# A streaming-encoder block: the residual placed in the output first, the last step added onto it by accumulating transfers

## The chip, the cores and the metric

The kernel runs on one core of one Trainium2 chip. The metric is the device time of one execution in microseconds. Times of the profile are those of one profiled execution, counted from the start of its span.

The engines are named as in the profile: PE multiplies matrices (PEld loads its weights), DVE is the vector engine, ACT the scalar engine, POOL is GpSimd, and SP mostly starts transfers. SPq, ACTq and POOLq are the DMA queues of the engines that issue the transfers.

## The reference, cut to what matters

```python
for l in range(DEPTH):                                   # one layer
    h = rmsnorm(x, norm_mix_pre[l])
    proj = h @ w_in[l]                                   # pool branch, GLU pair, two gates
    branch_a, branch_b = pool_mixer(...), conformer_conv(...)
    merged = sigmoid(g_a) * branch_a + sigmoid(g_b) * branch_b
    x = x + rmsnorm(merged @ w_o[l], norm_mix_post[l])   # x1 below
    h = rmsnorm(x, norm_mlp_pre[l])
    f = square(relu(h @ w_up[l])) @ w_down[l]
    x = x + rmsnorm(f, norm_mlp_post[l])                 # the output
# rmsnorm(y, g) = y * rsqrt(mean(y*y) + 1e-6) * g
```

The input has 2048 tokens of 1024 channels in float32; the MLP is 4096 wide. The value of `x` after the first half of the layer is called x1. The output is x1 plus the normalised MLP result, times a gain per channel.

The kernel doesn't normalise x1 ahead of `w_up`. Since relu and square pass a positive factor of a token through as its square, it multiplies unnormalised x1 and puts the token's factor into the last normalisation instead. That last normalisation then needs, per token, a function of the mean square of x1: the code calls it the floor (the "MLP scale"), which stands in for the 1e-6.

## The kernel before, in words

**Tiling.** A tile is 128 x 1024 float32 (512 KB). Tokens are split into two blocks of 1024 (`b`), each block into two halves of 512 (`t`), each half into four groups of 128 tokens (`g`). Up to the MLP, data lie with channels on the partitions. The last product, `down`, has tokens on the partitions: its results are 128 tokens by 512 channels (`m` is the half of the channels, `h` the pair of groups; one accumulator tile holds two groups of 128 tokens side by side for one `m`).

**Products.** Every large product is computed as seven products of halves instead of eight (index `i` from 1 to 7; some need sums of weight tiles and of token tiles, some don't), and every operand is split into a rounded high part (`wh`, a cast on ACT) and a low part (`wl`, a subtraction on DVE), with three matmuls each. In `down` the 4096 inputs are taken in four slabs; slab 3 is the last (`LAST`). A job of `down` is one index `i` for one block `b`: 24 matmuls for each of the two `h`.

**Stages.** Input projections and convolution for block 0, then 1; merge and `w_o`; `up` for block 0 and, after `w_o` of block 1, `up` for block 1; then `down`, slab 0 to slab 3. In the profile `down` runs from about 1541 us to the end, and its last slab from about 2000 us.

**What sets the order.** The Python program is run once and gives each engine its own list of instructions; waits on semaphores tie the lists together. Work beside the matmuls is written as generators in lanes: `Lane(rate, ...)` takes `rate` steps of its generators at each call of `bg()`, which comes once for each `h` of a job; `yield n` in a generator waits `n` steps. `with tc.high_priority(...)` puts instructions ahead in the engine's list.

**The parts the change touches.**

- `mlp_scale` (line 1312) and `scales` (1578): while `up` of block 1 runs, x1 is read back with channels on the partitions (`fo<-x1d`), squared on ACT (line 579), added on DVE, and summed over the channels by matmuls against a column of 1/1024 (`rb<-inv_d,fo`, line 458). The result is the floor of each group of tokens.
- `last_weights` (line 1559): also beside `up` of block 1, the weights of the last slab are read, the sums for i = 5, 6, 3, 7 are formed and stored (`wsum`), and the low part of every weight tile is computed and stored (`lows`). In the last slab `part` (line 1634) loads the tile, casts its high part, and loads its low part (`wl<-lows`).
- `turned` (line 1771): beside slabs 0 to 2, x1 is read (two loads per piece, `tr<-x1d`), transposed by DVE in squares of 32 x 32 (line 1785), and written with tokens as rows to an internal buffer (four stores per piece, `x1t<-tr`). All six go through POOL's queue. There are 16 pieces.
- `Finish`: one per (block, half). When an accumulator is ready, ACT sums its squares (line 1812), and DVE multiplies it by the gain (`big<-big,ws`). When all four are ready, a chain of small DVE operations (`root`, `root_dve`) gives the factor per token; for each group of 128 tokens the row tile of x1 is fetched (`big<-x1t`), and DVE computes y times factor plus x1 in two halves (line 1832), and the row tile is stored (`put`, line 1839: POOL's queue for block 0, SP's for block 1). The last `Finish` does the same in `at_end` as its matmuls end, with stores of 256 KB on SP's queue (line 1888).

The program is built with `dynamic_dma_scratch_size=1024` (line 2046), the space it sets aside for the descriptors of transfers that POOL issues. Both versions have this line.

Of the kernel before, what the change touches and what calls it, by code (L numbers as in the profile page):

```python
# [67 lines left out]
def block_kernel(  # L68
# [124 lines left out]
    fd, x1t = {}, {(b, t): dram("x1t", (T, D)) for b in range(NB) for t in (0, 1)}  # L193
# [958 lines left out]
    floor = {}  # L1152
# [158 lines left out]

    def mlp_scale(b, buf):

        st = None
        for t in (0, 1):
            sq = Squares(buf)
            for c in range(0, CPS, 2):
                x = [mk(*buf) for _ in (0, 1)]
                for i in (0, 1):
                    load(x[i], x1d[b, c + i, t])  # L1320
                yield 1
                sq.add(x[0])
                sq.add(x[1])
            yield 1
            ss = sq.total()
            yield 2
            if st is None:
                st = root_psum()
            root_acc(st, ss, inv_d, t * G)
        yield 1  # L1330
        m = small("sa", 2 * G)
        nc.vector.tensor_scalar(
            m, st[:, : 2 * G], EPS, SQ * EPS**0.5, op0=ALU.add, op1=ALU.mult
        )
        e = p_const.tile([P, 2 * G], F32, tag=f"e{b}", name=f"e{b}")
        mul(e, m, m)
        for t in (0, 1):
            floor[b, t] = e[:, t * G : (t + 1) * G]
        yield
# [230 lines left out]
    def last_weights():  # L1570
# [11 lines left out]
        keys = [(o, i) for o in (0, 1) for i in DOWN]  # L1582
        for (o, i), got in ahead_by_one(keys, fetch_one):
# [15 lines left out]
            hi, lo = split(t, *TR)  # L1599
            yield 1  # L1600
            lows[i, o] = dram("lows")
            load(lows[i, o], f32(lo))

    def scales():
        for b in range(NB):
            yield from mlp_scale(b, (p_fo, "fo"))


    def weights_down(s):
# [27 lines left out]
        def part(i, o):  # L1637
            with tc.high_priority(offset=AHEAD):
                if s < LAST:
                    return split_w(source(i, o))  # L1640
                if (i, o) in wsum:
                    t = mk(p_wr, "wr")
                    load(t, wsum[i, o])
                else:
                    t = source(i, o)
                hi, lo = mk(p_wh, "wh", F32R), mk(p_wl, "wl", F32R)
                nc.scalar.copy(hi, t)
                load(f32(lo), lows[i, o])
                return hi, lo
# [120 lines left out]

    def turned():
        for b in range(NB):
            for t in (0, 1):
                to = x1t[b, t].rearrange("(n tb i) (q k j) -> n q i tb k j", n=2, i=32, q=4, j=32)
                for c in (0, 2):
                    for n in (0, 1):
# [7 lines left out]
                        yield 4  # L1784
# [9 lines left out]
                        yield  # L1794

# [3 lines left out]
    class Finish:  # L1799
# [16 lines left out]
        def gain(self, m, h):  # L1816
# [3 lines left out]
            row = gains[0][:, m * T : (m + 1) * T].unsqueeze(1).to_broadcast([P, 2, T])  # L1820
            mul(two(y), two(y), row)

        def root(self, lo, hi):
            ss = small("st", hi - lo)
            add(ss, self.ss[:, lo:hi], self.ss[:, G + lo : G + hi])
            return root_dve(ss, floor[self.b, self.t][:, lo:hi], 1.0 / D)

        def cell(self, g, r, y):
            x = self.x[g]
            for m in (0, 1):  # L1830
                s = slice(m * T, (m + 1) * T)
                nc.vector.scalar_tensor_tensor(x[:, s], y[m], r, x[:, s], op0=ALU.mult, op1=ALU.add)

        def parts(self, g):
            s = slice(g % 2 * T, (g % 2 + 1) * T)
            return [self.ready[m, g // 2][:, s] for m in (0, 1)]

        def put(self, g):
            (nc.gpsimd if self.b == 0 else nc.sync).dma_start(
                out[self.b, self.t, g], self.x[g]  # L1840
            )

        def steps(self, lag):
# [5 lines left out]
            for g in range(3):  # L1849
                self.fetch(g)  # L1850
# [3 lines left out]
            for g in range(G):  # L1854
                if g + 3 < G:
                    self.fetch(g + 3)
                self.cell(g, r[:, g : g + 1], self.parts(g))
                self.put(g)
                yield

        def last_steps(self):
            for n, k in enumerate(((1, 0), (1, 1))):
# [4 lines left out]
                self.fetch(2 * n)  # L1867
                yield
                self.fetch(2 * n + 1)
                yield  # L1870

        def at_end(self, h, c, ps):
            y = tr()
            halves = [slice(i * T, (i + 1) * T) for i in (0, 1)]

            def arrive(gg):
                s = halves[gg]
                mark(add(c[:, s], c[:, s], ps[gg]))
                self.squares(0, h, c[:, s], gg)
                mul(y[:, s], c[:, s], gains[0][:, :T])  # L1880

            def leave(g, r):
                to = out[self.b, self.t, g]
                part = [y[:, halves[g % 2]], self.ready[1, h][:, halves[g % 2]]]
                x = self.x[g]
                for m, s in list(enumerate(halves))[::-1]:
                    nc.vector.scalar_tensor_tensor(x[:, s], part[m], r, x[:, s], op0=ALU.mult, op1=ALU.add)
                    load(to[:, s], x[:, s])
# [63 lines left out]
    for n, (s, i, b) in enumerate(jobs):  # L1952
# [17 lines left out]
        if n == 1:  # L1970
            lanes.append(Lane(2, turned()))
# [82 lines left out]
```

## Time and profile before

| what | value |
|---|---|
| median of 3 runs | 2153.35 us (2151.98 to 2154.61) |
| profiled execution | 2155.38 us, of it span 2153.6 us and 1.8 us around it |
| mean granted clock of PE | 0.996 |
| PE busy | 2130.3 us, 99% of the span |
| DVE busy | 1717.0 us, 80% |
| ACT busy | 1024.5 us, 48% |
| POOL busy | 74.8 us, 3% |
| PE's last matmul ends | 2141.0 us |
| DVE's last operation ends | 2150.2 us |

An engine is busy while it runs an instruction of its own; issuing a transfer counts as busy for POOL but not for SP. A row of a timeline gives the start, the length, the engine, the line of the kernel, the operation, what it writes and reads, the count, and in brackets the idle time ahead of it with what ended it. A row of DMA issues gives the queue, the count, the size of each transfer and the median time from its issue to its landing.

### The profile page before, as it was taken

What the parts mean: (1) busy time and instruction counts of PE and PEld (TensorE: products, weight loads), DVE (VectorE), ACT (ScalarE), POOL (GpSimd) and SP (SyncE); (2) the same over time, 40 slices, a digit from 0 to 9 for tenths busy, and PEclk for the clock granted to TensorE, in tenths of its full rate; (3) what the DMA queues carried; (4) which work ended last, traced back from release to release, by engine and by line L of the source; (5) the groups of instructions that cost most, each with busy time, mean ns of one, the idle gap of its engine ahead of it and who ended that gap; (6) DMA issues with size and microseconds to landing.
All of it is one profiled execution on the core that took longest, in us unless ns stands there. A gap on an engine that the chain in (4) does not pass through costs nothing.

```text
span 2153.6 us, 24989 instructions
## 1 busy us (share of the span) xinstructions
PE 2130.3 (99%) x9424; PEld 1758.8 (82%) x9424; DVE 1717.0 (80%) x1669; ACT 1024.5 (48%) x1109; POOL 74.8 (3%) x131
## 2 busy tenths in 40 slices
PE   9999999999999999999999999999999999999997
PEld 8788888888888888888888888888888888888886
DVE  8999788999779999998768766876745667688558
ACT  6444453334534755446645676665544322223343
POOL 0000000000000000000000000000011111100000
PEclk9999999999999999999999999999999999999999
DMA  4789999688897787335596787995977657564568
GB/s 178 262 309 329 342 356 317 223 292 290 307 345 282 248 305 292 149 118 223 200 382 211 248 293 268 338 334 192 366 264 264 246 197 253 180 221 164 198 228 338
DMA packets 164617, 568.04 MB, mean 264 GB/s; under 512 B 19984, under 2 KB 24208, under 8 KB 164496
## 3 DMA queue, kind: packets, MB, share of 16 engines
q1 hardware_dynamic: 142736, 490.93, 63.4%
q10 hardware_dynamic: 12672, 46.14, 5.5%
q0 software_dynamic: 9088, 29.37, 3.9%
q8 instruction: 74, 1.21, 0.2%
q14 instruction: 47, 0.39, 0.1%
HBM read 370.71 MB, written 195.65 MB: 263 GB/s over the span
## 4 chain that ended last, share of the span: by engine, by line
PE 85%; DVE 8%; DMA 3%; issue 2%; ACT 1%; SPq 0%; DVEq 0%; ACTq 0%
PE up L252 28%; PE down L1708 26%; PE wo L252 7%; PE glu L252 4%; PE B L252 4%; PE gb L252 4%; PE A L252 4%; PE ga L252 3%; DVE y L910 3%; PE pool L252 3%; PE rb L1708 1%; DVE tr L120 1%; DVE wl L123 1%; DMA kept<-ws 1%; PE rb L458 1%
## 5 line engine op out<-in xcount | busy, mean ns | idle before, releaser
L252 PE MATMUL up<-big,wh 128*128 128x512 f32 x1792 | 481.0, 390 | 1.4 <-DVE big L123 0.8
L252 PEld LDWEIGHTS up<-big,wh 128*128 128x128 f32 x1792 | 335.7, 188 | 72.5 <-DVE big L123 1.1
L209 ACT CAST wh<-wr 128x1024 fp32r<-128x1024 f32 x167 | 175.6, 1052 | 305.8 <-PE up L252 70.0
L910 DVE SCALAR_TENSOR_TENSOR y<-v,cst,y 128x1024 f32<-128x1024 f32 x240 | 307.1, 1280 | 2.4
L1708 PE MATMUL down<-wh,fo 128*128 128x512 f32 x756 | 290.3, 389 | 0.3 <-DVE st L120 0.3
L1708 PE MATMUL down<-wh,tr 128*128 128x512 f32 x744 | 289.4, 389 | 0.0
L252 PE MATMUL up<-big,wl 128*128 128x512 f32 x896 | 276.0, 389 | 0.0
L209 ACT CAST wh<-ws 128x1024 fp32r<-128x1024 f32 x124 | 130.6, 1053 | 212.7 <-PE up L252 73.8
L1708 PE MATMUL down<-wl,fo 128*128 128x512 f32 x740 | 227.8, 389 | 0.0
L252 PEld LDWEIGHTS up<-big,wl 128*128 128x128 f32 x896 | 168.1, 188 | 35.0
L123 DVE TENSOR_TENSOR wl<-ws,wh 128x1024 fp32r<-128x1024 f32 x116 | 141.6, 1220 | 48.5 <-ACT wh L209 46.9
L1688 ACT CAST fo<-tr 128x1024 fp32r<-128x1024 f32 x86 | 89.9, 1052 | 176.8 <-DMA tr<-fd 121.0
L1708 PEld LDWEIGHTS down<-wh,fo 128*128 128x128 f32 x756 | 141.9, 188 | 30.4 <-issue 0.9
L1708 PEld LDWEIGHTS down<-wh,tr 128*128 128x128 f32 x744 | 139.6, 188 | 28.9
L1708 PEld LDWEIGHTS down<-wl,fo 128*128 128x128 f32 x740 | 138.9, 188 | 28.9
L123 DVE TENSOR_TENSOR wl<-wr,wh 128x1024 fp32r<-128x1024 f32 x111 | 135.2, 1219 | 25.6 <-ACT wh L209 22.6
L123 DVE TENSOR_TENSOR tr<-tr,fo 128x1024 fp32r<-128x1024 f32 x86 | 103.8, 1221 | 56.4 <-ACT fo L1688 55.9
L120 DVE TENSOR_TENSOR big<-big,down 128x1024 f32<-128x1024 f32 (+1 forms) x79 | 94.0, 1190 | 60.4 <-PE down L1708 60.0
L252 PE MATMUL gb<-big,wh 128*128 128x512 f32 x448 | 121.6, 393 | 0.0
L252 PE MATMUL glu<-big,wh 128*128 128x512 f32 x432 | 117.5, 393 | 3.2 <-ACT tr L408 3.2
L252 PE MATMUL wo<-big,wh 128*128 128x512 f32 x448 | 120.2, 390 | 0.0
L252 PE MATMUL ga<-big,wh 128*128 128x512 f32 x448 | 119.7, 389 | 0.0
(208 smaller groups left out, 3423.9 us busy)
## 6 DMA issues: line engine op xcount, KB each, us to landing
tr<-fd SPq DMA_DIRECT2D x110, 512.0 KB, 5.7
wl<-kept SPq DMA_DIRECT2D x67, 512.0 KB, 4.8
kept<-wl SPq DMA_DIRECT2D x66, 512.0 KB, 5.7
wr<-w_up SPq DMA_DIRECT2D x64, 512.0 KB, 4.6
wr<-w_down SPq DMA_DIRECT2D x62, 512.0 KB, 4.7
wr<-w_in SPq DMA_DIRECT2D x56, 512.0 KB, 5.6
fd<-tr ACTq DMA_DIRECT2D x54, 512.0 KB, 3.7
fd<-tr SPq DMA_DIRECT2D x48, 512.0 KB, 3.1
```

The source lines that it names most:

```text
L120: return nc.vector.tensor_tensor(o, a, b, op=ALU.add)
L123: return nc.vector.tensor_tensor(o, a, b, op=ALU.subtract)
L209: nc.scalar.copy(hi[:, :n], src[:, :n])
L252: i = nc.tensor.matmul(ps, w[wp][:, (at + k) * P : (at + k + 1) * P], rhs[k][xp], start=start and n == 0, stop=stop and n == len(order) - ...
L458: nc.tensor.matmul(st[:, at + g : at + g + 1], ss[:, g * P : (g + 1) * P], inv_n, start=start is None or (start and g == 0), stop=stop, sk ...
L910: nc.vector.scalar_tensor_tensor(acc, v[:, k : k + TB], wk, acc, op0=ALU.mult, op1=ALU.add)
L1688: nc.scalar.copy(hi, t)
L1708: i = nc.tensor.matmul(ps[gg], cells[j][xp][:, c * T + at : c * T + at + P], w[j][wp][:, c * T : (c + 1) * T], start=start and first, stop ...
```

## The change

x1 is turned into rows directly in the output tensor, and what the last step computes is added onto it by transfers that accumulate, so that row tiles of x1 are neither kept in an internal buffer nor fetched for the last step.

- `turned` writes into `out`. Its lane takes 3 steps instead of 2, and it waits 3 steps instead of 4 ahead of the transposition. After the four pieces of a (block, half), the new `row_squares` loads the four row tiles of 512 KB back from `out` on SP's queue, and ACT sums their squares along the rows (`accum_out`); two small DVE operations make the floor of it.
- `mlp_scale` and `scales` are gone: 16 loads, 16 squares, the additions and the 4 groups of matmuls.
- `last_weights` keeps only the sums for i = 5, 6, 3, 7. The low parts of the last slab are computed where they are used (`split_w`: cast on ACT, subtraction on DVE) instead of loaded.
- `Finish` has no row tiles. `gain` keeps the squares only. `over(m, h, r)` multiplies an accumulator tile by factor and gain in one operation per group of tokens (128 x 512), and one transfer on POOL's queue adds the tile of 512 KB, 256 rows of 2 KB, onto `out`. There are 16 such transfers in place of the 12 stores of 512 KB and the 8 of 256 KB; the last `Finish` uses them too, at the very end.
- The lags of the lanes of the last step change (1, 0, 1 in place of 0, 1, 0; the last lane takes 3 steps instead of 2).

```diff
@@ last_weights
-        keys = [(o, i) for o in (0, 1) for i in DOWN]
+        keys = [(o, i) for o in (0, 1) for i in DOWN if i in (5, 6, 3, 7)]
...
-            hi, lo = split(t, *TR)
-            yield 1
-            lows[i, o] = dram("lows")
-            load(lows[i, o], f32(lo))
-
-    def scales():
-        for b in range(NB):
-            yield from mlp_scale(b, (p_fo, "fo"))
@@ part
-                hi, lo = mk(p_wh, "wh", F32R), mk(p_wl, "wl", F32R)
-                nc.scalar.copy(hi, t)
-                load(f32(lo), lows[i, o])
-                return hi, lo
+                return split_w(t)
@@ turned
+    def rows(b, t):
+        return out[b, t].rearrange("g p d -> (g p) d")
...
-                to = x1t[b, t].rearrange("(n tb i) (q k j) -> n q i tb k j", n=2, i=32, q=4, j=32)
+                to = rows(b, t).rearrange("(n tb i) (q k j) -> n q i tb k j", n=2, i=32, q=4, j=32)
...
-                        yield 4
+                        yield 3
...
+                yield 2
+                yield from fin[b, t].row_squares()
@@ Finish
-        def fetch(self, g):
-            self.x[g] = mk(*BIG)
-            load(self.x[g], x1t[self.b, self.t][g * P : (g + 1) * P])
+        def row_squares(self):
+            sx = small("sx", G)
+            tiles = []
+            for g in range(G + 1):
+                if g < G:
+                    tiles.append(mk(*TR))
+                    load(tiles[g], rows(self.b, self.t)[g * P : (g + 1) * P])
+                    yield 1 + (g == 0)
+                if g:
+                    x = tiles[g - 1]
+                    nc.scalar.activation(x, x, AF.Square, accum_out=sx[:, g - 1 : g])
+            m = small("sm", G)
+            k = SQ * EPS**0.5
+            nc.vector.tensor_scalar(m, sx, k / D, k * EPS, op0=ALU.mult, op1=ALU.add)
+            self.floor = mk(p_gain, f"e{self.b}{self.t}", F32, (P, G))
+            mul(self.floor, m, m)
...
-            row = gains[0][:, m * T : (m + 1) * T].unsqueeze(1).to_broadcast([P, 2, T])
-            mul(two(y), two(y), row)
+
+        def over(self, m, h, r):
+            y, s = self.ready[m, h], slice(m * T, (m + 1) * T)
+            for gg in (0, 1):
+                part = y[:, gg * T : (gg + 1) * T]
+                nc.vector.scalar_tensor_tensor(
+                    part, part, r[:, gg : gg + 1], gains[0][:, s], op0=ALU.mult, op1=ALU.mult
+                )
+            to = out[self.b, self.t, 2 * h : 2 * h + 2].rearrange("g p d -> p g d")[:, :, s]
+            nc.gpsimd.dma_start(to, two(y), accum_op=ALU.add)
...
-            for g in range(G):
-                if g + 3 < G:
-                    self.fetch(g + 3)
-                self.cell(g, r[:, g : g + 1], self.parts(g))
-                self.put(g)
-                yield
+            for h in (0, 1):
+                for m in (0, 1):
+                    self.over(m, h, r[:, 2 * h : 2 * h + 2])
+                    yield
@@ at_end
-                    arrive(gg)
-                    if h:
-                        if gg:
-                            r = self.root(2, 4)
-                            for g in (2, 3):
-                                leave(g, r[:, g - 2 : g - 1])
...
+                    mark(add(c[:, s], c[:, s], ps[gg]))
+                    self.squares(0, h, c[:, s], gg)
+                    if gg:
+                        r = self.root(2 * h, 2 * h + 2)
+                        for m in (1, 0):
+                            self.over(m, h, r)
@@ the main program
-    then(lambda: lanes.extend([Lane(1, scales()), Lane(1, last_weights())]), octs[1])
+    then(lambda: lanes.extend([Lane(1, last_weights())]), octs[1])
...
-                lanes += [Lane(3, fin[0, 0].steps(0), fin[1, 0].steps(1), fin[0, 1].steps(0)), Lane(2, fin[1, 1].last_steps())]
+                lanes += [Lane(3, fin[0, 0].steps(1), fin[1, 0].steps(0), fin[0, 1].steps(1)), Lane(3, fin[1, 1].last_steps())]
...
-            lanes.append(Lane(2, turned()))
+            lanes.append(Lane(3, turned()))
```

**How the order of instructions moves.** The end of POOL's list, before: behind the last piece of `turned`, eight stores of whole row tiles (names with a number are tiles; `big` is one pool of tiles, an accumulator or a row tile).

```order
L133 DMA x1t_188<-tr_14505 32x8x128 x4
L1839 DMA out<-big_15822 128x1024
L1839 DMA out<-big_15824 128x1024
L1839 DMA out<-big_15826 128x1024
L1839 DMA out<-big_15848 128x1024
L1839 DMA out<-big_16133 128x1024
```

And in the changed kernel, the same place: sixteen accumulating transfers, of which the first eight stand here.

```order
L133 DMA out<-tr_14556 32x8x128 x4
L1805 DMA out<-big_12803 128x2x512
L1805 DMA out<-big_12645 128x2x512
L1805 DMA out<-big_12830 128x2x512
L1805 DMA out<-big_12674 128x2x512
L1805 DMA out<-big_12873 128x2x512
L1805 DMA out<-big_12714 128x2x512
L1805 DMA out<-big_12909 128x2x512
L1805 DMA out<-big_12744 128x2x512
```

POOL now issues everything that leaves for the output in the last slab, each transfer with 256 rows where the stores before had 128.

DVE's list in the last slab of the changed kernel, where the first of these transfers get their tiles (`down_...` and `rb_...` are results of PE, `wl_...` low parts of weights, `sy_...` the factors, `ws_15045` the gain):

```order
L120 TENSOR_TENSOR big_12714<-big_12714,down_15284 128x1024
L1801 SCALAR_TENSOR_TENSOR big_12803<-big_12803,sy_15698,ws_15045 128x512 x2
L1801 SCALAR_TENSOR_TENSOR big_12645<-big_12645,sy_15698,ws_15045 128x512 x2
L123 TENSOR_TENSOR wl_15786<-wr_15783,wh_15785 128x1024
L1801 SCALAR_TENSOR_TENSOR big_12830<-big_12830,sy_15698,ws_15045 128x512 x2
L123 TENSOR_TENSOR wl_15890<-wr_15887,wh_15889 128x1024
L123 TENSOR_TENSOR tr_15904<-tr_15904,big_15906 128x1024
L120 TENSOR_TENSOR big_12744<-big_12744,rb_15310 128x512
L120 TENSOR_TENSOR big_12744<-big_12744,rb_15311 128x512
L1801 SCALAR_TENSOR_TENSOR big_12674<-big_12674,sy_15698,ws_15045 128x512 x2
```

Four tiles of the first `Finish` become ready within some ten operations, and the subtractions for the low parts now stand among them. In PE's list, 217 matmuls follow the product that the first row adds.

DVE's list at the very end, before:

```order
L504 SCALAR_TENSOR_TENSOR s_3307_16373<-s_3306_16371,sa_16359 128x2
L504 SCALAR_TENSOR_TENSOR sy_16375<-s_3307_16373,sy_16369 128x2
L1887 SCALAR_TENSOR_TENSOR big_16322<-big_12233,sy_16375,big_16322 128x512
L1887 SCALAR_TENSOR_TENSOR big_16322<-tr_16326,sy_16375,big_16322 128x512
L1887 SCALAR_TENSOR_TENSOR big_16324<-big_12233,sy_16375,big_16324 128x512
L1887 SCALAR_TENSOR_TENSOR big_16324<-tr_16326,sy_16375,big_16324 128x512
```

And in the changed kernel, behind the addition of PE's last result:

```order
L120 TENSOR_TENSOR st_16165<-ss_1845_8578 128x2
L492 SCALAR_TENSOR_TENSOR sa_16167<-st_16165,e_3031_14955 128x2
L499 TENSOR_SCALAR sy_16169<-sa_16167 128x2
L126 TENSOR_TENSOR s_3206_16171<-sy_16169 128x2
L126 TENSOR_TENSOR s_3207_16173<-s_3206_16171,sa_16167 128x2
L504 SCALAR_TENSOR_TENSOR s_3208_16175<-s_3207_16173 128x2
L504 SCALAR_TENSOR_TENSOR sy_16177<-s_3208_16175,sy_16169 128x2
L126 TENSOR_TENSOR s_3210_16179<-sy_16177 128x2
L504 SCALAR_TENSOR_TENSOR s_3211_16181<-s_3210_16179,sa_16167 128x2
L504 SCALAR_TENSOR_TENSOR sy_16183<-s_3211_16181,sy_16177 128x2
L1801 SCALAR_TENSOR_TENSOR big_12027<-big_12027,sy_16183,ws_15045 128x512 x2
L1801 SCALAR_TENSOR_TENSOR big_12428<-big_12428,sy_16183,ws_15045 128x512 x2
```

Behind PE's last result the addition, the chain of the factor and four operations remain, as before; each pair of the four now gives one transfer of 512 KB on POOL's queue where before each single one gave a store of 256 KB on SP's.

More of the change, by code (lines that the diff above doesn't have):

```diff
@@ L192, in block_kernel @@
     )
-    fd, x1t = {}, {(b, t): dram("x1t", (T, D)) for b in range(NB) for t in (0, 1)}
+    fd = {}
     def col(i):
@@ L1310, in out_proj @@
         return roots(1)
[L1312 to L1320, printed above, removed]
-                yield 1
[L1322 to L1338, printed above, removed]
-        yield
     def mlp_up(b, parts):
@@ L1825, in root @@
             add(ss, self.ss[:, lo:hi], self.ss[:, G + lo : G + hi])
[L1826 to L1841, printed above, removed]
+            return root_dve(ss, self.floor[:, lo:hi], 1.0 / D)
         def steps(self, lag):
@@ L1866, in last_steps @@
                 yield
[L1867 to L1870, printed above, removed]
         def at_end(self, h, c, ps):
[L1873 to L1888, printed above, removed]
+            self.ready[0, h] = c
             def after(gg):
+                s = slice(gg * T, (gg + 1) * T)
                 with tc.high_priority(offset=URGENT):
[L1892 to L1901 removed]
+                    mark(add(c[:, s], c[:, s], ps[gg]))
[4 more added lines that the diff above has]
+                            self.over(m, h, r)
             return after
```

11 lines of the change are left out of this document (1 added, 10 removed).

## The prediction

> **What bounds the kernel now.** I read the page first, for the engines' shares, and the span cut into stages behind it. The columns of the cut are the length, then busy time and count of PE, PEld, DVE, ACT and POOL, the granted clock, the DMA engines' busy share and GB/s.
>
> ```profile
> PE 2130.3 (99%) x9424; PEld 1758.8 (82%) x9424; DVE 1717.0 (80%) x1669; ACT 1024.5 (48%) x1109; POOL 74.8 (3%) x131
> q0 software_dynamic: 9088, 29.37, 3.9%
> ...
> 1240.00:1541.00 301.00, 300.82 (x1342) 248.97 (x1342) 221.08 (x195) 190.12 (x193) 1.45 (x2) 1.00 0.81 292
> 1541.00:1800.00 259.00, 259.00 (x1144) 214.48 (x1143) 155.14 (x133) 97.96 (x98) 39.38 (x63) 1.00 0.73 258
> 2000.00:2100.00 100.00, 100.00 (x443) 82.80 (x442) 53.28 (x59) 39.08 (x59) 0.00 (x0) 1.00 0.58 211
> 2100.00:2141.00 41.00, 40.39 (x176) 32.47 (x174) 39.18 (x71) 16.76 (x36) 4.35 (x8) 1.00 0.98 369
> 2141.00:2153.60 12.60, 0.01 (x1) 0.00 (x0) 8.76 (x26) 0.72 (x2) 0.00 (x0) 0.58 0.61 237
> ```
>
> PE is the bound, at the full clock (1.00) and with no gap from 1541 to 2100 us. So work taken from another engine gains nothing before PE's end, which I call P (2141.0 us here); a gain can only be matmuls removed, waits of PE removed, or a shorter stretch behind P, 12.6 us now. A loss can come from new waits of PE, or from anything that is not done when PE is. PE's waits in the last slab, 2000 us to the end:
>
> ```profile
> PE down L1708 <- DMA wl<-lows: 0.3, 1, 0.3
> PE down L1708 <- DVE st L120: 0.3, 1, 0.3
> ```
>
> The stretch behind P, in order of time:
>
> ```profile
> 2140.39 0.61 PE L1708 MATMUL rb<-wl,big 128*128 128x512 f32 x2
> ...
> 2141.20 0.68 DVE L120 TENSOR_TENSOR big<-big,rb 128x512 f32<-128x512 f32 x1
> ...
> 2141.97 0.63 ACT L1812 ACTIVATE ws<-big 128x512 f32<-128x512 f32 x1 [1.46 <-DVE sy L504]
> 2142.51 0.19 ACT L1812 ACTIVATION_READ_ACCUMULATOR ws<-big 128x1 f32 x1
> ...
> 2143.97 6.54 SPq L129 DMA_DIRECT2D out<-big  x8
> ...
> 2149.41 0.75 DVE L1887 SCALAR_TENSOR_TENSOR big<-tr,sy,big 128x512 f32<-128x512 f32 x1
> ...
> out<-big SPq DMA_DIRECT2D x8, 256.0 KB, 2.1
> ```
>
> DVE ends at 2150.16 (P+9.15), the last small store lands about 2.2 us behind that, and some 1.2 us remain to the span's end at 2153.6. The stores leave as DVE makes them: DVE is the limit of this stretch, not the transfers.
>
> **PE's part of the change.** `mlp_scale` had four groups of matmuls in `up`:
>
> ```profile
> 1341.21 0.39 PE L252 MATMUL up<-big,wl 128*128 128x512 f32 x1
> 1341.44 0.95 PE L458 MATMUL rb<-inv_d,fo 128*128 128x1 f32 x8
> 1342.24 1.65 PE L252 MATMUL up<-big,wh 128*128 128x512 f32 x6
> ```
>
> A group pushes the next matmul from 1341.44 to 1342.24, 0.80 us. Four are 3.2 us, and the wait for `wl<-lows` is 0.3 more. I take **P 3.5 us earlier**. Bounds: 0 (a freed slot is lost to a later wait) and 3.8 (the wait for `st` goes too).
>
> **Edits at nothing.** The dropped squares, sums, casts and transfers of `mlp_scale` and `last_weights` lie beside a PE that is busy 300.82 of 301.00 us. In the last slab DVE gets 18 subtractions for the low parts and loses the 14 multiplications by the gain and four half ones:
>
> ```profile
> L123 DVE TENSOR_TENSOR wl<-wr,wh 128x1024 fp32r<-128x1024 f32 x111 | 135.2, 1219 | 25.6 <-ACT wh L209 22.6
> ...
> L126 DVE TENSOR_TENSOR big<-big,ws 128x1024 f32<-128x1024 f32 x14 | 17.0, 1222 | 5.2 <-ACT ws L1812 5.2
> L1832 DVE SCALAR_TENSOR_TENSOR big<-big,sy,big 128x512 f32<-128x512 f32 x24 | 16.6, 745 | 0.1
> L126 DVE TENSOR_TENSOR tr<-big,ws 128x512 f32<-128x512 f32 x4 | 2.7, 685 | 0.0
> ```
>
> 18 x 1.22 = 22.0 against 17.0 + 2.7 = 19.7: 2.3 us more over the slab, covered by the 46.7 us in which DVE is idle between 2000 and 2100 us. The large multiply-adds stay 32. If the cover were gone (DVE is busy 39.18 of 41.00 us in the stretch after), each late low part would hold PE by at most its 1.22 us.
>
> **New work in slabs 0 to 2.** `row_squares` puts 16 loads of 512 KB on SP's queue between the loads of token and weight tiles, each waiting for stores of `turned`, and 16 squares on ACT in front of casts that PE needs. What is queued behind them are cells of later jobs. PE never waits from 1541 to 2100 us now, so a gain is excluded. The loss is bounded above by each of the four rounds holding one job for a store's median landing (6.1 us, shown below), 24 us. Counting DVE's and ACT's operations between a result of PE and the matmul that uses the next cell, I find margins of 0.6 us and more at most places and some two that come about 1 us late: an estimate of **+2**, and 0 to 6 for the range.
>
> **The sixteen accumulating transfers.** This term decides. Before, POOL's queue shows how much it holds. Rows of POOL's timeline: three of `turned`'s stores (256 rows of 512 B each), then the fourth; and four stores of the last slab (128 rows of 4 KB):
>
> ```profile
> 1552.57 1.77 POOL L133 DMA_DIRECT2D x1t<-tr  x3 [13.12 <-DVE tr L1785]
> 1558.75 0.59 POOL L133 DMA_DIRECT2D x1t<-tr  x1 [4.41 <-DMA wr<-w_down]
> ...
> 1611.44 1.76 POOL L133 DMA_DIRECT2D x1t<-tr  x3 [9.22 <-DVE tr L1785]
> 1614.19 0.59 POOL L133 DMA_DIRECT2D x1t<-tr  x1 [0.99 <-issue]
> ...
> 1908.63 1.75 POOL L133 DMA_DIRECT2D x1t<-tr  x3 [14.15 <-DVE tr L1785]
> 1915.49 0.58 POOL L133 DMA_DIRECT2D x1t<-tr  x1 [5.11 <-issue]
> ...
> 2101.37 0.58 POOL L1839 DMA_DIRECT2D out<-big  x1 [185.30 <-DVE big L1832]
> ...
> 2105.46 0.53 POOL L1839 DMA_DIRECT2D out<-big  x1 [0.90 <-DVE big L1832]
> ```
>
> The three go out together in 1.8 us, though the fourth depends on nothing that the three don't. It starts 6.18, 2.75 and 6.86 us after the first. Landing of these stores of 128 KB (first row), of POOL's transfers of x1, mostly `turned`'s loads of 256 KB (second), and of its larger ones:
>
> ```profile
> DMA to landing us min/median/max: 2.4/6.1/7.8
> ...
> DMA to landing us min/median/max: 2.9/3.5/8.9
> ...
> out<-big POOLq DMA_DIRECT2D x8, 512.0 KB, 8.1
> x1d<-big POOLq DMA_DIRECT2D x8, 512.0 KB, 5.9
> ```
>
> So the fourth starts when the first has landed, 0.35 us later (2.75 - 2.4): the queue holds 3 x 256 = 768 row reads and not 1024. Four stores of 128 rows go out in a row. Now an accumulating transfer of 256 rows has to read the tile and what lies in `out`: 512 reads. One fits; two are 1024, just what did not fit. I conclude that **the sixteen run one at a time**. Beside this stands the Trainium skill, "Collectives: The Full Stack", section "The bandwidth ceiling: the fold count and why AG ≠ RS ≠ AR": a reduce emits two read descriptors per chunk where a copy emits one, both on the same ring; it says this of collectives, and no run here yet shows it of a kernel's own transfer.
>
> One at a time, each costs c, from issue to landing plus 0.35. POOL's queue moved 29.37 MB in 3.9% of 2153.6 us, 84.0 us: 350 GB/s, so 128 KB take 0.37 us and 512 KB 1.50. From the least landing, 2.4 - 0.37 = 2.0 us are fixed. A copy of 512 KB would be 3.5, a second read makes 5.0, and c = 5.35 with nothing beside it. Beside the last slab's loads copies land later, 5.9 to 8.1; I take c = 6.0 for the eight that run before P and 5.35 for the rest. By the price of "DMA: Bandwidth & Descriptors" in the Trainium skill, section "Anatomy of one DMA — SWDGE (gpsimd) path" (2.0 us and 436 GB/s), c would be an estimated 4.75 and the sum below 17 instead of 32; the slower 350 GB/s are this trace's own.
>
> The first four accumulates become ready together: PE's product ahead of them is complete 217 matmuls before P, 49 us at 443 per 100.00 us; the addition and two multiplications of 0.67 follow, so the first starts at about P-46. By DVE's order later ones come at P-42 to P-28, P-13 to P-7, and the last four at P+0.4, +1.7, +6.7, +8.1: always sooner than the queue gets to them. The end is then -46 + 8 x 6.0 + 8 x 5.35 - 0.35 + 1.2 = **P+45.7** instead of P+12.6: +33.1.
>
> **The sum**: 33.1 - 3.5 + 2.0 = +31.6, on the profiled 2155.4 us: 2187.0. The median of the runs shown lies 2.0 below the profiled time; for it I say **2185 us**. Bounds of c: 3.85 (the second read costs nothing), which ends at -46 + 61.6 + 0.85 = P+16.5, +0.4 in all without stalls; and 9.95 (8.1 + 1.5 + 0.35), P+114, about 2259. The rows near 5 us bear the lower half better: nothing competes behind P.
>
> **The rivals.**
>
> *Three in flight* (a read of the destination doesn't count against the queue, or it counts bytes): for it, three transfers of 256 rows did go out together; against it, the fourth shows a limit, and an accumulate asks for more than a copy. DVE's stretch behind P gets shorter: addition 0.68 from P+1.7, square 0.82, the factor's ten operations 2.0, four multiplications 2.7: DVE ends at P+8.1 instead of P+9.15. Then issue 0.2, landing X of 512 KB, and 1.2 to the end: P+9.5+X. With X = 5.0, P+14.5, +1.9 - 3.5 + 0 to 2: 2153.8 to 2155.8 profiled, about 2153 by the median. Not slower; it decides if c is under 3.6 or two or more overlap.
>
> *The tail shrinks.* Three in flight, and X = 2.9, what a 256 KB copy took at best: P+12.4, -0.2 - 3.5 = -3.7, with the `st` wait gone -4.0: 2151.4 profiled, 2149 by the median. For it, behind P nothing else moves; against it, 512 KB copies of this queue landed after 5.9 and 8.1 in the median.
>
> *SP's queue stalls PE.* The accumulates overlap, but the row loads hold up weights in slabs 0 to 2 by 6 us or more: 2157 to 2165. For it, SP works in order and the loads wait for POOL's stores; against it, cells are fetched at least one job ahead, 48 matmuls or 10.8 us at the rate above.
>
> **How the numbers follow.** One at a time 0.64, three in flight 0.22, shorter tail 0.08, stalls alone 0.06. A measurement of this kernel tells 0.2%, 4.3 us, from no change. Faster than that: nearly all of the shorter tail's 0.08, since it lies at that edge, and a little of three in flight: 0.09. No change: the rest of three in flight and the one-at-a-time cases with c under 4.1: 0.24. Slower: 0.67. The range reaches down to three in flight, 2151, and up to c = 7.3 throughout (P+71.7, +59.1 - 3.5 + 2 = 2213 profiled), 2211. One at a time alone: 2168 to 2211.
>
> **What would show it.** POOL's timeline in the last slab: each accumulate a landing after the one before, the last issued some 35 us behind P, with DVE, ACT and PE idle there; DVE's end at P+8. PE's root matmuls gone from `up`, P 1 to 4 us earlier. New waits of PE in 1541 to 2100 us would be the row loads' share. The forecast is wrong if two accumulates are issued within 2 us of each other while a third is in flight, or if a landing takes under 3.5 us.

## The result, and the profile after

The changed kernel takes 2204.85 us (median of 4 runs, 2202.09 to 2205.53), the kernel before 2153.98 us in the same comparison: a ratio of 1.0229, 95% interval 1.0215 to 1.0242. It is slower by 51 us. The forecast was 2185 us with a range of 2151 to 2211.

The page of the changed kernel, and its span cut into stages (length, then busy time and count of PE, PEld, DVE, ACT and POOL, clock, DMA share, GB/s):

```profile
PE 2126.9 (97%) x9392; PEld 1755.5 (80%) x9392; DVE 1688.2 (77%) x1643; ACT 1014.4 (46%) x1111; POOL 89.7 (4%) x139
q0 software_dynamic: 12288, 33.56, 6.3%
...
1240.00:1541.00 301.00, 300.82 (x1327) 248.84 (x1327) 192.96 (x165) 165.04 (x167) 1.45 (x2) 1.00 0.64 233
1541.00:1800.00 259.00, 255.51 (x1122) 209.87 (x1121) 150.24 (x132) 103.71 (x112) 35.37 (x56) 1.00 0.75 269
2100.00:2138.00 38.00, 38.00 (x169) 31.49 (x168) 32.40 (x60) 16.54 (x37) 7.21 (x6) 1.00 0.66 106
2138.00:2203.00 65.00, 3.42 (x16) 2.49 (x14) 9.43 (x28) 1.45 (x4) 10.86 (x9) 0.56 0.59 80
```

PE does 3.4 us less work than before (2126.9 against 2130.3), but has lost 3.5 us in 1541 to 1800 us, where it had no gap. Of the 65 us behind 2138 us, PE is busy for 3.42 and DVE for 9.43; in the rest only transfers move, and over the whole stretch they reach 80 GB/s. The ends of PE and DVE, from the timeline:

```profile
2140.81 0.61 PE L1666 MATMUL rb<-wl,big 128*128 128x512 f32 x2
...
2146.14 2.74 DVE L1801 SCALAR_TENSOR_TENSOR big<-big,sy,ws 128x512 f32<-128x512 f32 x4
```

PE ends at P = 2141.42 (2141.01 before), DVE at 2148.88 (P+7.5), the span at 2202.7 (P+61.3, before P+12.6). So 48.7 of the 49.2 us between the two profiled executions (2204.57 and 2155.38) lie behind P, and P itself has hardly moved. What fills them, from POOL's timeline, the first two of the sixteen accumulates and the last two, with the rows of their line:

```profile
2095.86 1.25 POOL L1805 DMA_DIRECT2D out<-big  x1 [153.61 <-DVE big L1801]
2102.77 1.22 POOL L1805 DMA_DIRECT2D out<-big  x1 [5.66 <-DVE big L120]
...
2188.70 1.21 POOL L1805 DMA_DIRECT2D out<-big  x1 [5.23 <-issue]
2195.16 1.21 POOL L1805 DMA_DIRECT2D out<-big  x1 [5.25 <-issue]
...
L1805 POOL DMA_DIRECT2D out<-big x16: 1197/1207/1253, 2095.9 to 2195.2; - x16
...
DMA to landing us min/median/max: 6.1/6.3/6.6
```

The starts are (2195.16 - 2095.86) / 15 = 6.62 us apart, a landing of 6.3 and 0.3 more. The page puts the gaps of the later ones down to "issue", which means that it saw no semaphore behind them. The reading is that POOL sits in the issue of a transfer until its queue has room; the runs below test it.

How PE's end came out the same: the last matmul of `up` and the first of `down` that reads slab 0's tiles, before (first two rows) and after, each row with the first and the last start of its group:

```profile
L252 PE MATMUL up<-big,wl x896: 387/389/402, 788.5 to 1540.9; 128*128 128x512 f32 x180
L1708 PE MATMUL down<-wh,big x180: 387/389/397, 1541.4 to 2134.5; 128*128 128x512 f32 x180
```

```profile
L252 PE MATMUL up<-big,wl x896: 388/389/397, 788.9 to 1537.0; 128*128 128x512 f32 x180
L1666 PE MATMUL down<-wh,big x180: 389/389/389, 1537.4 to 2134.9; 128*128 128x512 f32 x180
```

`up` ends 3.9 us earlier (counted from its first row, it is 4.3 us shorter: 1537.0 - 788.9 = 748.1 against 1540.9 - 788.5 = 752.4); `down` takes 2141.42 - 1537.4 = 604.0 us instead of 2141.01 - 1541.4 = 599.6, 4.4 more. PE's waits in `down` of the changed kernel (us in total, times, longest) name most of it; before, there were 0.6 us:

```profile
PE down L1666 <- DVE tr L123: 3.4, 4, 1.5
PE down L1666 <- DVE big L120: 0.3, 1, 0.3
```

A caution for what follows: executions of kernels that are alike up to there end `up` anywhere from 1532.4 to 1540.2 us. That spread lies ahead of `up`: the first row above starts at 784.3 to 792.0 us in them, and `up` then lasts 748.1 to 748.5 us in each. Single profiled executions can be compared by stages, but their totals only within some 4 us either way.

### The profile page after: what moved, and what is told of

Its sections match the earlier page's. It is cut to its first block, busy times and chain, and to the rows that moved or that the text cites. A ratio compares the mean times of both kernels' runs of the same rounds, so it can differ in the third digit from the quotient of the medians.

```text
span 2202.7 us, 24790 instructions
## 1 busy us (share of the span) xinstructions
PE 2126.9 (97%) x9392; PEld 1755.5 (80%) x9392; DVE 1688.2 (77%) x1643; ACT 1014.4 (46%) x1111; POOL 89.7 (4%) x139
## 3 DMA queue, kind: packets, MB, share of 16 engines
q8 instruction: 74, 1.21, 0.2%
## 4 chain that ended last, share of the span: by engine, by line
PE 75%; DVE 12%; issue 5%; DMA 4%; ACT 1%; POOL 0%; SPq 0%; POOLq 0%; DVEq 0%; ACTq 0%
PE up L252 27%; PE down L1666 24%; PE wo L252 7%; DVE y L910 5%; PE B L252 4%; PE A L252 4%; PE gb L252 3%; PE glu L252 3%; DVE wl L123 2%; DVE tr L120 1%; PE rb L1666 1%; PE pool L252 1%; DMA kept<-ws 1%; DVE ws L123 1%; DMA kept<-wl 1%
## 5 line engine op out<-in xcount | busy, mean ns | idle before, releaser
L209 ACT CAST wh<-wr 128x1024 fp32r<-128x1024 f32 x185 | 194.6, 1052 | 384.5 <-PE up L252 90.1
L123 DVE TENSOR_TENSOR wl<-wr,wh 128x1024 fp32r<-128x1024 f32 x129 | 157.1, 1218 | 41.7 <-ACT wh L209 39.6
```

The source lines that it names most:

```text
L123: return nc.vector.tensor_tensor(o, a, b, op=ALU.subtract)
L209: nc.scalar.copy(hi[:, :n], src[:, :n])
```

## The experiments

The question after the result was whether the accumulates run one at a time because of the room on POOL's queue, as the prediction had it, and what made each dearer than forecast. A second was which of the other parts gave or took what on PE.

### Stores in place of accumulates

```diff
-            nc.gpsimd.dma_start(to, two(y), accum_op=ALU.add)
+            nc.gpsimd.dma_start(to, two(y))
```

> The changed kernel with its sixteen transfers of the last step as plain stores of the same shape (256 rows of 2 KB, POOL's queue), so that x1 is not added and the output is the normalised MLP result alone. Theory (what counts on POOL's queue is row reads; a store has 256 where an accumulate has 512): up to three in flight, no backlog, the last store leaves right behind DVE's last multiplication at P+7.5; span end P+7.5+0.2+4 to 6+1.2, a time of 2156 to 2159 us, and the fourth store of a burst again waits for the first. Rival (transfers of this shape onto this tensor follow one another whatever they do): one every 4 to 6 us, 2165 to 2200 us.

2156.2 us, beside 2157.0 for the kernel before (one run of each, and so in the next three runs). POOL's timeline and the landings:

```profile
2096.26 0.74 POOL L1805 DMA_DIRECT2D out<-big  x1 [153.65 <-DVE big L1801]
2097.59 0.73 POOL L1805 DMA_DIRECT2D out<-big  x1 [0.59 <-DVE big L1801]
...
2149.69 0.72 POOL L1805 DMA_DIRECT2D out<-big  x1 [0.61 <-DVE big L1801]
...
DMA to landing us min/median/max: 3.1/3.4/6.3
...
q0 software_dynamic: 10240, 33.56, 4.5%
```

Each store now starts when DVE has made its tile, the last one 8 us behind P. Neither the shape nor the tensor makes them follow one another: the rival falls. The rows also price the addition in this pair of runs. The queue's share of the 16 engines is 4.5% of 2154.4 us here, 96.9 us, and 6.3% of 2202.7, 138.8 us, with accumulates: 41.9 us for sixteen, 2.6 us of all engines for each. (A share is rounded to 0.1%, which leaves about 0.1 us either way for each transfer.) In landing it is 6.3 against 3.4 us, with 1.21 instead of 0.72 us of that in the issue.

### Accumulates of 128 rows

```diff
-            to = out[self.b, self.t, 2 * h : 2 * h + 2].rearrange("g p d -> p g d")[:, :, s]
-            nc.gpsimd.dma_start(to, two(y), accum_op=ALU.add)
+            for gg in (0, 1):
+                nc.gpsimd.dma_start(
+                    out[self.b, self.t, 2 * h + gg][:, s], y[:, gg * T : (gg + 1) * T], accum_op=ALU.add
+                )
```

> Each of the sixteen accumulating transfers cut in two, one per group of 128 tokens (128 rows of 2 KB, 256 KB): 32 accumulates with 256 reads each by the theory. Theory (room for some 768 reads): three in flight as with three plain stores of 256 rows, no backlog behind P, end at about P+14, 2156 to 2160 us. Rival (an accumulating transfer waits for the one before, whatever its size): 32 x (2.0 + 1.5 + about 1.4 of issue and turnaround) = 32 x 4.9 = 157 us from P-45.6, about 2255 us.

2159.5 us. The first four and the last two of the 32, and their landings:

```profile
2092.82 2.75 POOL L1805 DMA_DIRECT2D out<-big  x3 [152.23 <-DVE big L1801]
2098.45 0.86 POOL L1805 DMA_DIRECT2D out<-big  x1 [2.88 <-DVE wl L123]
...
2149.21 0.86 POOL L1805 DMA_DIRECT2D out<-big  x1 [1.04 <-issue]
2151.86 0.87 POOL L1805 DMA_DIRECT2D out<-big  x1 [1.79 <-issue]
...
DMA to landing us min/median/max: 4.0/5.3/8.7
```

Three go out at once and the fourth 5.6 us behind the first, the picture that three stores of 256 rows gave before. An accumulate of 128 rows behaves on this queue like a store of 256. The same bytes are added, and 45 us of the loss are gone. Behind P (2139.09) there are still 18.7 us, since the queue is still full there: the last accumulate starts 5 us after DVE's last multiplication.

### More room on the queue

Two runs. The second needs space for descriptors, so both have one buffer less for raw weights.

```diff
-    p_wr = pool("pwr", 5)
+    p_wr = pool("pwr", 4)
# the second run also:
-    nc = bacc.Bacc("TRN2", target_bir_lowering=False, num_devices=1, dynamic_dma_scratch_size=1024)
+    nc = bacc.Bacc("TRN2", target_bir_lowering=False, num_devices=1, dynamic_dma_scratch_size=4096)
```

> The changed kernel with four buffers for raw weight tiles instead of five; this frees the space for the next run and is its control. Both theories: accumulates still one at a time at 6.6 us; 2205 us plus what later weight loads cost PE (0 to 10 us), since the accumulates start with the last slab's results.

> As the run before, with 4096 instead of 1024 as the space set aside for the descriptors of POOL's transfers (dynamic_dma_scratch_size); nothing else differs. Theory (the queue's room serialises): four times the room holds several accumulates, they overlap, no backlog behind P: about 48 us less than the run before, 2157 to 2167 us. Also the fourth store of turned's bursts goes out with the first three. Rival (accumulates are serial for another reason): the same as the run before within 3 us, with 6.6 us from one to the next.

2225.7 us and 2182.8 us. The missing buffer cost PE more than expected, 19.6 us (P = 2161.04 in the control), all of it ahead of `up`, whose first matmul starts at 807.4 instead of 787.6 us. It is in both runs, and it is why the second lies above the 2157 to 2167 us expected of it. POOL's timeline of the control, one burst of `turned` and the first accumulates:

```profile
1570.96 1.78 POOL L133 DMA_DIRECT2D out<-tr  x3 [15.46 <-DVE tr L1746]
1578.87 0.58 POOL L133 DMA_DIRECT2D out<-tr  x1 [6.13 <-DMA big<-fd]
...
2115.48 1.25 POOL L1805 DMA_DIRECT2D out<-big  x1 [153.16 <-DVE big L1801]
2122.17 1.22 POOL L1805 DMA_DIRECT2D out<-big  x1 [5.44 <-DVE big L120]
```

And with the larger space:

```profile
1573.63 2.34 POOL L133 DMA_DIRECT2D out<-tr  x4 [16.15 <-DVE tr L1746]
...
2117.51 2.54 POOL L1805 DMA_DIRECT2D out<-big  x2 [154.05 <-DVE big L1801]
2121.30 1.18 POOL L1805 DMA_DIRECT2D out<-big  x1 [1.24 <-DVE big L1801]
...
DMA to landing us min/median/max: 6.3/7.9/11.8
...
q0 software_dynamic: 12288, 33.56, 5.8%
```

The fourth store of a burst goes out with the first three, the accumulates leave as DVE makes them, and the stretch behind P is 17.8 us (P = 2163.20) instead of 62.9. One number in the program's setup, the only difference between the two kernels, takes back 43 us (48 were expected): the room on the queue is the cause. The queue's share of the engines is smaller too: 5.8% of 2181.0 us is 126.5. Against the 96.9 with stores that is 1.9 us for each addition, where the changed kernel had 2.6.

### Full rows

```diff
-        def over(self, m, h, r):
+        def over(self, g, r):
+            x, part = mk(*BIG), slice(g % 2 * T, (g % 2 + 1) * T)
+            for m in (1, 0):
+                s = slice(m * T, (m + 1) * T)
+                nc.vector.scalar_tensor_tensor(
+                    x[:, s], self.ready[m, g // 2][:, part], r, gains[0][:, s], op0=ALU.mult, op1=ALU.mult
+                )
+            nc.gpsimd.dma_start(out[self.b, self.t, g], x, accum_op=ALU.add)
```

> The changed kernel with each accumulate covering one group of 128 tokens in full rows: 128 rows of 4 KB, the same 512 KB, DVE writing into a fresh tile. Theory of the room (it counts rows read, 256 here): up to three in flight, no backlog behind P, the stretch behind P 14 to 18 us, about 2157 to 2161 us. On what an accumulate's own time follows: if bytes, one that goes alone lands after about 6.1 us as the changed kernel's did; if rows, after about 4.0 us as the least of the 256 KB ones with 128 rows. Rival (room counts bytes): one at a time as in the changed kernel, about 2205 us.

2162.3 us (one run), beside 2154.7 for the kernel before. Two neighbours of POOL's timeline behind P, and the landings:

```profile
2144.88 0.88 POOL L1804 DMA_DIRECT2D out<-big  x1 [7.08 <-DVE big L1801]
2146.20 0.87 POOL L1804 DMA_DIRECT2D out<-big  x1 [0.44 <-DVE big L1801]
...
DMA to landing us min/median/max: 5.3/6.9/11.6
...
q0 software_dynamic: 10240, 33.56, 5.7%
```

Sixteen accumulates of 512 KB, 1.3 us apart where DVE gives them so, though none lands in less than 5.3, and no backlog: the room counts rows, not bytes. The stretch behind P (2144.48) is 16.0 us, 3.4 more than with stores, since the last two of 512 KB have to be added behind everything else. The least landing, 5.3 us, lies nearer the 6.1 of the changed kernel's 512 KB than the 4.0 of half the bytes: an accumulate's own time follows mostly its bytes, a little its rows. Its share of the engines, 5.7% of 2160.5 us or 123.1, is 1.6 us above a store's for each.

### Low parts computed, alone

The kernel before with `last_weights` and `part` as in the change (the first two pieces of its diff), nothing else.

> The kernel before with one part of the change: the low parts of the last slab computed instead of loaded, last_weights keeping only the sums. Theory (DVE's idle time hides the 18 subtractions): within 1.5 us of before, the wait of 0.3 us for the loaded low part gone. Rival (with the multiplications by the gain still there, DVE has both in the last 41 us, where it was busy 39.18 of 41.00): low parts come late, PE waits for DVE wl in the last 25 us, 4 to 7 us slower.

Ratio 1.0090, interval 1.0063 to 1.0117: slower, the rival's side, and by more than it said. PE's waits in `down` and in `up`, and the end of the last slab:

```profile
PE down L1701 <- DVE st L120: 6.0, 1, 6.0
PE down L1701 <- DVE big L120: 1.1, 1, 1.1
...
PE up L252 <- ACT tr L408: 2.0, 2, 1.8
...
PE rb L458 <- DVE fo L120: 0.8, 1, 0.8
...
2100.00:2157.00 57.00, 49.17 (x204) 39.52 (x203) 54.88 (x94) 22.74 (x49) 4.34 (x8) 0.94 0.66 249
```

DVE is busy 54.88 of 57.00 us and late with everything: PE stands 6.0 us behind an accumulator that DVE has not added up yet. In the whole change PE has no wait from 2000 us on. The multiplications by the gain go there at the same time, which is the likely reason; no run takes out these two parts alone. P is 2155.19 in this execution, 14 us later than before. Of that, `down` has 9.1 (608.7 us against 599.6). `up` is 3.1 us longer (755.5 against 752.4), and PE's waits there, for ACT and for the sums of `mlp_scale` on DVE, are 2.6 us more than before. The other 2.0 lie ahead of `up`, within the spread named above. The execution is the shortest of four (2169.9 to 2180.1), so it shows only part of what the others lost.

### The MLP scale along rows, alone

The kernel before with `mlp_scale` gone, and `turned` and `row_squares` as in the change, on the internal buffer `x1t` instead of the output.

> The kernel before with one other part: the MLP scale summed along rows (row tiles loaded back from the internal buffer, ACT squares with a sum), no matmuls for it; turned as in the change but into the internal buffer; stores and low parts as before. Theory (what the four root groups give back, the shifted cells on DVE take again): 3.2 us less in up, and PE's two waits of 1.5 us for DVE tr in slabs 0 to 2 as in the changed kernel: within 1.5 us of before. Rival (those waits come from what is done to the output tensor): no such waits, 3 us faster.

Ratio 1.0010, interval 1.0000 to 1.0020. The theory holds: `up` has no root matmuls, and the waits of the changed kernel are there without any accumulate and without the output tensor:

```profile
PE down L1674 <- DVE tr L123: 3.4, 4, 1.5
```

`down` takes 2143.45 - 1538.5 = 605.0 us, 5.4 more than before. What the part saves in `up` it pays in `down`. The part holds both `row_squares` and the new steps of `turned`; this run doesn't say which of the two PE pays for.

### The transpositions one call later

The version with accumulates of 128 rows, and a `yield 1` as the first line of `turned`.

> As the run with accumulates of 128 rows, with turned started one call of the lanes later, nothing else. Theory (PE's two waits for DVE tr come from where the transpositions and the cells meet in DVE's list): the waits are gone, about 3 us less than that run, 2155 to 2158 us, against before within 3 us. Rival (they come from the row loads on SP's queue): the waits stay.

Ratio 1.0030, interval 1.0019 to 1.0042, a median of 2163.7 us. It did not work. The profiled execution, 2157.9 us, is the second shortest of ten (2156.1 to 2165.6), so it can't show what most of them lost. PE's waits in `down`:

```profile
PE down L1666 <- ACT fo L1646: 1.5, 1, 1.5
PE down L1666 <- DVE tr L123: 1.1, 2, 0.8
PE down L1666 <- DVE big L123: 0.9, 2, 0.4
```

The two waits of 1.5 us for DVE are gone, so those did depend on when `turned` takes its steps. But no transposition stands at them. The rows ahead of the second one in the changed kernel, from the timelines of ACT, DVE and PE:

```profile
1787.25 1.05 ACT L209 CAST wh<-wr 128x1024 fp32r<-128x1024 f32 x1 [17.82 <-PE down L1666]
1788.21 1.05 ACT L1646 CAST fo<-tr 128x1024 fp32r<-128x1024 f32 x1
...
1788.34 1.22 DVE L123 TENSOR_TENSOR wl<-wr,wh 128x1024 fp32r<-128x1024 f32 x1 [0.99 <-ACT wh L209]
...
1794.02 3.49 DVE L123 TENSOR_TENSOR tr<-tr,fo 128x1024 fp32r<-128x1024 f32 x3
...
1795.29 0.50 PE L1666 MATMUL down<-wh,tr 128*128 128x512 f32 x1 [1.48 <-DVE tr L123]
```

ACT stands 17.82 us at the cast of a weight tile, a wait put down to PE, with the casts of token cells behind it in its list; DVE then works without a gap and has the cell ready just before PE starts. Before, ACT's longest wait of this kind in slabs 0 to 2 was 6.7 us, and in this run, without the two waits, it is 9.4. So the order on ACT is the better candidate; what moved it isn't shown. The 3.5 us of waits that are left are for ACT and DVE together, and 3.1 of them lie between 1566 and 1603 us, ahead of the first row load at 1634.6: they can't be work of `row_squares`.

### Accumulates for twelve tiles, the last four as before

From the version just shown; the last `Finish` fetches its row tiles (from the output) and stores through SP as in the kernel before.

```diff
+        def fetch(self, g):
+            self.x[g] = mk(*BIG)
+            load(self.x[g], rows(self.b, self.t)[g * P : (g + 1) * P])
...
         def last_steps(self):   # gain, multiplication, fetch, as before
         def at_end(self, h, c, ps):   # as before
```

> As the run before, but the last Finish works as in the kernel before: row tiles of x1 fetched (from the output tensor), added by DVE, eight stores of 256 KB on SP's queue behind PE's end; the other twelve tiles leave as 24 accumulates of 128 rows. Theory (the 18.7 us behind PE's end in the run with 128 rows are POOL's queue; before it were 12.6): the stretch behind PE's end is 12 to 13 us again, 6 us less than the run before: 2149 to 2152 us, 2 to 5 us faster than before. Rival (the late accumulates still land behind SP's stores, or the fetches crowd the queue): no more than 2 us gained on the run before.

Ratio 0.9999, interval 0.9990 to 1.0009; 9 us less than the run before, measured beside it, but not the 2 to 5 us under the kernel before that were expected. The profiled execution ends PE at 2143.43 and the span at 2155.7:

```profile
2142.82 0.61 PE L1666 MATMUL rb<-wl,big 128*128 128x512 f32 x2
...
2151.62 0.75 DVE L1862 SCALAR_TENSOR_TENSOR big<-tr,sy,big 128x512 f32<-128x512 f32 x1
```

The stretch behind P is 12.3 us, as in the kernel before. So accumulates do no harm where nothing waits for them and the queue has room; at the very end stores are cheaper. `down` takes 605.7 us, with 4.6 us of waits, so the 4 us of `up` are lost again. No version beats the kernel before.

### The MLP scale from the fetched rows

The kernel before without `mlp_scale`; the row tiles that the last slab fetches anyway are fetched one result earlier, and ACT squares them there. This part is no part of the change; it asks if the 4 us of `up` can be kept.

```diff
+        def row_square(self, g):
+            nc.scalar.activation(junk[0], self.x[g], AF.Square, accum_out=self.sx[:, g : g + 1])
...
                 self.gain(*k)
+                self.fetch(n)
                 yield
```

> The kernel before with only the MLP scale changed, and elsewhere than in the change: no matmuls for it in up; the row tiles that the last step fetches anyway are fetched one result earlier and squared along the rows on ACT in the last slab; turned, low parts and stores as before. Theory (the 4.0 us that the changed kernel gains in up are lost again by the row loads and squares in slabs 0 to 2): down takes 599.6 us as before, 4 us faster in all, 0.998. Rival (the squares delay ACT's casts or the earlier fetches crowd SP's queue in the last slab): PE waits there, within 1.5 us of before or slower.

Ratio 1.0061, interval 1.0047 to 1.0075. `up` is 4.1 us shorter, as in the other runs, but PE waits once for 3.7 us behind a low part that SP's queue now loads too late, and `down` takes 604.0 us, 4.4 more than before. The stretch behind P grows to 22 us, since DVE's work of the last steps comes later too:

```profile
PE down L1673 <- DMA wl<-lows: 3.7, 1, 3.7
```

From 1541 to 2100 us PE has no gap here. The run with the scale along rows has the changed kernel's waits there. So the 3.5 us that the changed kernel loses there come from `turned` and `row_squares`, not from what `mlp_scale` leaves behind. The profiled execution (2162.2 us) is the shortest of five; the other four, 2167.6 to 2169.1, lost more than it shows.

## Why the prediction was right, and where its numbers were off

**One at a time: right.** The prediction counted rows on POOL's queue, 768 fit and 1024 don't, and gave an accumulate 512. Four runs agree: accumulates of half the rows, of full rows, or with four times the space overlap, and stores of the same shape never queue. No row shows that an accumulate's row counts exactly twice. The runs bound it: more than 1.5 times a store's row, since two accumulates of 256 rows don't fit where three stores do (768 / 512), and less than 2.7, since three of 128 rows do where four stores don't (1024 / 384). The Trainium skill, "Collectives: The Full Stack", section "The bandwidth ceiling: the fold count and why AG ≠ RS ≠ AR", states for collectives that a reduce emits two read descriptors per chunk where a copy emits one. These bounds agree with it.

**The time of one: the term that was mis-sized.** The prediction had 5.35 us alone, 1.5 of it for the second read, and 6.0 beside the last slab's loads. Measured: 6.62, the same before P as behind it (2095.86 to 2142.33 is 7 x 6.64). The copy part was sound: stores of 512 KB landed after 3.1 at least and 3.4 in the median, forecast 3.5. The second read was not: an accumulate lands 2.9 us later than the store of its shape, not 1.5, and half a microsecond of that is the issue. What the rest is made of stays open. The engines' time for the addition is 2.6 us here but 1.9 with the larger space and 1.6 with full rows, near the forecast, so it is no fixed price. And the allowance for the loads beside it was not needed. One of the landings that it was taken from, 5.9 us, is of stores at 747 to 788 us, not of the last slab. Sixteen times the difference, 105.9 - 90.8 = 15.1 us, is nearly the whole distance from P+45.7 to P+61.3. With the 1.9 us by which PE ends later than forecast, that accounts for the step from 2187.0 to the profiled 2204.57. The other price in the prediction, an estimated 4.75 us worked out from "DMA: Bandwidth & Descriptors" of the Trainium skill, section "Anatomy of one DMA — SWDGE (gpsimd) path", was further off; the section gives a plain transfer's cost and says nothing of an accumulate's.

**When they start, and DVE's end: right.** The first accumulate at P-45.6 (forecast P-46), DVE's end at P+7.5 (P+8.1). Every later tile was ready before the queue got to it.

**PE's part: right in its pieces, off in their balance.** `up` itself is 4.3 us shorter, 1.1 for each group of root matmuls (forecast 0.80), and ends 3.9 earlier; `down` lost 4.4 (forecast 2.0 of new waits, less 0.3). Net PE ended 0.4 us later instead of 1.5 earlier. The upper bound of 6 held. The two large waits are both for cells on DVE that came 1.5 us late; the prediction had "some two" of about 1 us, and not the smaller losses around them. That the row loads make these waits isn't shown.

**Edits at nothing: right only for the change as a whole.** With the 18 subtractions PE has no new wait in the last slab, as the balance of 2.3 us had it. The run with this part alone shows that the cover is thin: with the gain's multiplications still there it costs 0.9%, though some of that arises in `up`.

**The rivals.** Three in flight did not happen, but the run with stores shows that its working was sound: stores land 3.4 us after their issue and end at P+12.6, and the version with full rows, whose accumulates do overlap, ends at P+16.0 against the P+14.5 of the prediction. The shorter tail is excluded by 5.3 us, the least landing of a 512 KB accumulate, where it asked for 2.9. The stall of PE by SP's queue did not show: PE's new waits name DVE, and with 4.4 us they stay below that rival's 6.

## What to carry to other kernels

A transfer that adds onto its destination is not a store with a free addition: here it took about twice the room on the issuing queue and almost twice the time to land (6.3 against 3.4 us for 512 KB), so count both before moving an add there, and look in the old trace for a burst on that queue whose later members start only when the first has landed. Where such transfers back up, halve their rows or enlarge the queue's space first; and keep them away from the end of the program, where their landing is on the path. Work that leaves a full PE at one stage is worth only what the stage that takes it over has free: here 3.9 us were saved in one and 4.4 lost in the other.

## What was not expected of the hardware

An accumulate of 512 KB in 256 rows, alone on its queue, landed 2.9 us later than a store of the same shape (6.3 against 3.4), where the bytes of a second read take 1.5 us at the rate that this queue showed. It landed after 6.1 to 6.6 us whether or not loads ran beside it. The DMA engines' time for the addition was 2.6 us there, but 1.9 where the same accumulates overlapped. The issue on POOL grows with the rows and with the addition: 0.53 us for a store of 128 rows, 0.72 for 256 rows, 0.87 for an accumulate of 128 rows, 1.21 for one of 256.
